# One encoder layer, two sequences: sequence 0's matrix memory takes the form of sequence 1's

## The chip, the cores and the metric

The kernel runs on one core of one Trainium2 chip. The metric is the time of one execution on the device, in microseconds (us). The time given for a kernel is the median of several runs. One more execution is taken with the hardware profiler; the page and the trace quoted here come from it.

## What is computed

The reference is one layer of a hybrid encoder over two independent sequences (`x_prompt`, `x_sample`) of 512 tokens and width 1024, all in float32. A half-step SwiGLU network is followed by a token-mixing block, a second SwiGLU network and a last RMSNorm. The mixing block feeds two branches from one projection: attention with 8 heads, and a bidirectional matrix memory (mLSTM) with 4 heads of width 128. Both are projected up, gated and merged:

```python
att = gqa_block_attention(aq, ak, av)
mem = mlstm_bidirectional(mq, mk, mv, gate_pre, mlstm_gate_bias, o_pre, mlstm_head_norm)
merged = jax.nn.sigmoid(g_att) * (att @ w_up_att) + jax.nn.sigmoid(g_mlstm) * (mem @ w_up_mlstm)
x = x + merged @ w_out
```

Unrolled over a whole sequence, one direction of one memory head is a masked score matrix with exponential decay weights, times the values, divided by a row normaliser:

```python
S_qk = jnp.einsum('bhtd,bhsd->bhts', qc, kc) * jnp.exp(D - m_t[..., None])
num = jnp.einsum('bhts,bhse->bhte', S_qk, vc) + w_inter[..., None] * jnp.einsum('bhtd,bhde->bhte', qc, C)
h = num / jnp.maximum(jnp.abs(den), jnp.exp(-m_t))[..., None]
```

The kernel forms the 512×512 weights of both directions directly, adds them, and multiplies by the values.

## The kernel before

**Arithmetic.** A float32 operand of a matmul is split into a high part (ScalarE, ACT: a copy that rounds) and a low part (VectorE, DVE: the difference), both in the type fp32r; `split` (L733, L734) does it for tiles, `split_w` (L284, L285) for weights. A product is then three matmuls: high·high, high·low, low·high. Each runs over 512 columns on TensorE (PE).

**The mixing block.** `mix(s, ...)` is a generator that runs once for each sequence s; it works with the tokens along the free axis, so that a head's q, k and values are 128-row tiles of 512 columns. A unit of work such as `mem_qk(h, j)` (q or k of head h), `att_gate(d)`, `merge_att(d)` or `mem_gate(d)` is a pair of a weight load and a computation; `go(...)` runs units in the order written, with loads ahead of computations. A scheduler then orders the instructions of each engine by their place in the code and by what is ready in its own model; inside `marks[0] = True` some instructions are pinned to the written order.

**One memory head, `mem_head(h)`.** For each of four row blocks i: three matmuls make the scores into a PSUM bank `pss` (L1309; two such banks); ACT makes five exponentials of decay rows (L1323); DVE multiplies scores and weights once for each direction (L1325). The decay rows come from DRAM by a DMA on SP's queue (L1088, `box<-ebuf`), and a masked copy `em` of them is made by an addition (L1091): on GpSimd (POOL) for heads 1 to 3 of sequence 0, on DVE otherwise. Then the normaliser is inverted and both directions are joined (L1336 ACT, L1337 and L1339 DVE). The result is four row tiles `Ts` of 128×512.

**Values, `mem_out(h)`.** The value product contracts over the columns of `Ts`, so they must be turned. Sequence 0 does it on PE: 16 transposes of 128×128 per head into `pst` (L1372), then `split`, then 12 matmuls into the bank `pso` (L1381). Sequence 1 does it without PE: `mem_blocks(h)` turns every 32×32 block in place on DVE (L1347, eight instructions per head), `mem_send` writes the blocks to DRAM in eight DMAs of 128 KB on POOL's queue (L1355, `tbuf`), and `mem_out` fetches four tiles `f` of 256 KB back in the turned order, also on POOL's queue (L1368). These are split and multiplied as above; an ACT copy (L1387) restores the order of the columns of `pso`. Then come the output gate (L1391), the sums of squares over a scratch row `turned_`, and the normed head into the tile `mem` (L1398).

**Order around it.** Sequence 1's four heads stand in one order written by hand: a head's scores, then units of other work, then that head's values. Sequence 0 runs a loop over the heads that puts units into a queue and takes them out with `fill`.

**Buffers.** `A(...)` takes one of seven equal large buffers; `att` (attention's output), `mem`, `Vm` (the values), `mg` (the gates), `kv` and `qT` live there. `F2()` takes one of four places for tiles of 128×512 (`f2`); attention's fetches, the scaled products of `mem_qk` of sequence 0 and the memory's fetches share them. Weights that are split live in four `w8` places, raw weights in four `wr` places. PSUM has banks `mm`, `pso`, `pss`, `pst`; merges and gates use `mm`.

Of the kernel before, what the change touches and what calls it, by code (L numbers as in the profile page):

```python
# [8 lines left out]
F32 = mybir.dt.float32  # L9
# [7 lines left out]
P = 128  # L17
# [9 lines left out]
def encoder(ctx, tc, I, outs):  # L27
# [837 lines left out]
    def mix(s, xh, xl, early=None, extra=None, after=None):  # L865
# [166 lines left out]

        def mem_qk(h, j):
            def done(pp):
                if j == 0 and not s:
                    t = wpool.tile([P, 4, S], F32R, tag="w8", bufs=4, name=nm("qk"))
                    qks[h] = [t[:, i] for i in range(4)]
                elif s:
                    t = mem[:, 2 + j] if h == 2 else wpool.tile([P, 2, S], F32R, tag="wr", bufs=4, name=nm("qk"))
                    qks.setdefault(h, []).extend(t[:, i] for i in range(2))  # L1040
                t = pp
                if not s:
                    t = F2()
# [40 lines left out]
        def mem_rows(h, d):  # L1084

            eb = T2(F32, "eb")
            eb3 = eb.rearrange("p (b s) -> p b s", b=4)
            nc.sync.dma_start(eb3, ebuf[d, :, h, :].partition_broadcast(P))  # L1088
            em = T2(F32, "eb")
            em3 = em.rearrange("p (b s) -> p b s", b=4)  # L1090
            (V_ if s or not h else G_).tensor_tensor(em3, eb3, tabs[3][:, d].unsqueeze(1).to_broadcast([P, 4, P]), op=ALU.add)  # L1091
            return eb3, em3

        def mem_scales():
# [246 lines left out]

        def mem_blocks(h, Ts):

            q = [wpool.tile([P, 8, 4, 32], F32, tag="wr", bufs=4, name=nm("qt")) for _ in range(2)]
            for i in range(4):
                for g in range(2):
                    V_.transpose(q[g][:, :, i, :],  # L1347
                                 Ts[i][0][:, g * 256:(g + 1) * 256].rearrange("p (n m) -> p n m", m=32))
            return h, q
# [9 lines left out]
        def mem_out(h, Ts):  # L1359
            moved = isinstance(Ts, int)  # L1360
            vm = Vm[0]
            po = PO()
            hs_ = slice(h * P, (h + 1) * P)
            turned = []
            for j in range(4 + 1):
                if j < 4 and moved:
                    p = F2()
                    mark(nc.gpsimd.dma_start(p, tbuf[Ts][4 * j:4 * j + 4].rearrange("c r a x -> (c r) (a x)")), True)  # L1368
                elif j < 4:
                    p = PT()  # L1370
                    for i in range(4):
                        nc.tensor.transpose(p[:, i * P:(i + 1) * P], Ts[i][0][:, j * P:(j + 1) * P], ident)  # L1372
                if j < 4:
                    ph, pl = T2(F32R), T2(F32R)
                    split(p, ph, pl)
                    turned.append((j, ph, pl))
                if j >= 1:
                    t, ph, pl = turned.pop(0)
                    with shifted(15):
                        for n, (a, b) in enumerate(((0, ph), (1, ph), (0, pl))):  # L1380
                            mark(nc.tensor.matmul(po, vm[:, a, t, hs_], b, start=(t == 0 and n == 0),  # L1381
                                                  stop=(t == 3 and n == 2)), True)
            h2 = T2()
            og = ogs[h]
            if moved:
                rows_ = T2()
                nc.scalar.activation(rows_.rearrange("p (i a m) -> p i a m", i=4, a=4),  # L1387
                                     po.rearrange("p (a i m) -> p i a m", i=4, a=4), AF.Copy)
                po = rows_
            nc.scalar.activation(h2, po, AF.Square)  # L1390
            V_.scalar_tensor_tensor(og, og, 1.0, po, op0=ALU.add, op1=ALU.mult)  # L1391
            turned_ = own[0] if own else F2()
            row = block_sums(h2, turned_)
            with shifted(60):
                rh = block_rstd(row, DM)
            with shifted(160):
                Rh = spread_rows(rh, turned_)
                V_.scalar_tensor_tensor(og, og, hn[:, h:h + 1], Rh, op0=ALU.mult, op1=ALU.mult)  # L1398
                split(og, mem[:, h, 0, :], mem[:, h, 1, :])

        if s:
            qk2, qk3 = [[mem_qk(h, j) for j in range(2)] for h in (2, 3)]
            ma = [merge_att(d) for d in range(KD)]
            marks[0] = True
            q = mem_blocks(0, mem_head(0))
            at = [mem_send(*q)]
            go(*mem_values(), *qk2)
            q = mem_blocks(1, mem_head(1))
            go(*qk3, ma[0], ma[1])
            mem_out(0, at[0])  # L1410
            at.append(mem_send(*q))
            q = mem_blocks(2, mem_head(2))
            go(att_gate(6), att_gate(7), ma[2], ma[3])
            mem_out(1, at[1])
            at.append(mem_send(*q))
            q = mem_blocks(3, mem_head(3))
            go(*ma[4:])
            mem_out(2, at[2])
            at.append(mem_send(*q))
            go(*[mem_gate(d) for d in range(EARLY)])  # L1420
            mem_out(3, at[3])
            marks[0] = False
        for h in range(HM if not s else 0):
            Ts = mem_head(h)
            if h == 0:
                go(*mem_values())
            queue.append(merge_att(2 * h))
            if h == 0:
                queue.append(merge_att(1))
            fill(1 + s)  # L1430
# [3 lines left out]
            if h:  # L1434
                queue.append(merge_att(2 * h + 1))
            fill(99)
# [559 lines left out]
```

## Time and profile before

| | |
|---|---|
| median of 3 runs | 2030.96 us (2028.93 to 2032.43) |
| the profiled execution | 2029.24 us |
| its span in the trace | 2027.5 us |
| mean granted clock of TensorE | 0.999 |
| DMA over the span | 482.11 MB, mean 238 GB/s |
| heads of sequence 0's memory in the trace | 797.5 to 955 us |
| heads of sequence 1's memory in the trace | 1188 to 1300 us |

The span is the stretch that the trace covers; the execution's own time is 1.7 us longer. In a row of the timeline the first two numbers are start and length in us, then engine, line, operation, output and inputs; what stands in brackets is the engine's idle time just before and what ended it. A busy time of PE counts matmuls from issue to a modelled end, so neighbouring ones overlap (a row says about 0.39 us where the next one starts 0.23 us later). A row that groups instructions ends with their busy time and the mean in ns, and behind the bar the idle time before them. "SPq" and "POOLq" are the queues' own instructions.

### The profile page before, as it was taken

To read this page: it belongs to the slowest core of one execution; us is meant where nothing else is said; L and a number is where in the kernel's file an instruction comes from. 1 tells how busy PE (TensorE), PEld (TensorE's weight loads), DVE (VectorE), ACT (ScalarE), POOL (GpSimd) and SP (SyncE) were. 2 spreads that over 40 slices of the span, in tenths; PEclk is the share of its full clock that TensorE was granted. 3 is DMA by queue.
4 is the path that set the end of the run, shared out by engine and by line. 5 is a ranking of instruction groups with operands and counts; after the bars stand their busy time and mean duration, and the time that the engine had idled before them with its cause. 6 is when DMAs were issued, how large, how long until landed. Compare 5 with 4: busy or idle time off the path is not lost.

```text
span 2027.5 us, 26874 instructions
## 1 busy us (share of the span) xinstructions
PE 2015.1 (99%) x9129; PEld 1661.4 (82%) x9129; DVE 1592.6 (79%) x2830; ACT 919.2 (45%) x1677; POOL 249.7 (12%) x313
## 2 busy tenths in 40 slices
PE   9999999999999999999999999999999999999998
PEld 7888888888888888788888878888888888888887
DVE  8989898896688788786566867377798988786797
ACT  7644444443224477653325655245444444442224
POOL 0243344201003000100120023011000000000001
PEclk9999999999999999999999999999999999999999
DMA  9778787799766766868657668867565655699753
GB/s 313 233 235 271 228 279 244 258 337 373 264 220 220 274 194 198 267 206 300 210 165 220 205 228 264 274 208 238 157 210 171 226 168 178 204 339 349 272 194 120
DMA packets 329546, 482.11 MB, mean 238 GB/s; under 512 B 23016, under 2 KB 196160, under 8 KB 328128
## 3 DMA queue, kind: packets, MB, share of 16 engines
q1 hardware_dynamic: 316352, 439.27, 64.9%
q0 software_dynamic: 12896, 40.86, 5.9%
q8 instruction: 72, 1.18, 0.2%
q14 instruction: 66, 0.54, 0.1%
q10 hardware_dynamic: 160, 0.27, 0.0%
HBM read 308.70 MB, written 171.61 MB: 237 GB/s over the span
## 4 chain that ended last, share of the span: by engine, by line
PE 94%; DVE 2%; DMA 2%; issue 1%; ACT 1%; SPq 0%; DVEq 0%; ACTq 0%
PE mm L856 16%; PE mm L380 11%; PE pso L380 11%; PE pst L380 11%; PE mm L650 9%; PE mm L842 5%; PE pss L380 5%; PE pss L650 4%; PE pst L650 4%; PE mm L821 3%; PE pso L650 3%; PE pss L1118 1%; PE pso L1165 1%; PE pso L1381 1%; PE pst L856 1%; PE pss L856 1%
## 5 line engine op out<-in xcount | busy, mean ns | idle before, releaser
L380 PE MATMUL pst<-xc,w 128*128 128x512 f32 x1056 | 253.8, 389 | 0.5 <-ACT t L415 0.5
L380 PEld LDWEIGHTS pst<-xc,w 128*128 128x128 f32 x1056 | 198.1, 188 | 42.0 <-ACT t L415 0.9
L380 PE MATMUL mm<-xc,w 128*128 128x512 f32 x972 | 229.8, 390 | 0.8 <-ACT t L388 0.8
L380 PEld LDWEIGHTS mm<-xc,w 128*128 128x128 f32 x972 | 181.8, 188 | 39.5 <-ACT t L388 1.9
L650 PE MATMUL mm<-rt,w 128*128 128x512 f32 x765 | 178.7, 389 | 0.0
L856 PE MATMUL mm<-xh,w 128*128 128x512 f32 x560 | 176.0, 391 | 0.0
L650 PEld LDWEIGHTS mm<-rt,w 128*128 128x128 f32 x765 | 143.5, 188 | 29.8
L338 ACT ACTIVATE w<-t 128x512 fp32r<-128x512 f32 x176 | 107.6, 628 | 130.7 <-issue 59.1
L339 DVE TENSOR_TENSOR w<-t,w 128x512 fp32r<-128x512 f32 x176 | 120.2, 701 | 31.7 <-ACT w L338 30.0
L380 PE MATMUL pso<-xc,f 128*128 128x512 f32 x528 | 127.1, 390 | 0.1
L380 PE MATMUL pss<-xc,w 128*128 128x512 f32 x528 | 126.8, 389 | 0.0
L380 PE MATMUL pso<-xc,w 128*128 128x512 f32 x528 | 126.8, 389 | 0.0
L856 PEld LDWEIGHTS mm<-xh,w 128*128 128x128 f32 x560 | 104.9, 188 | 21.8
L380 PEld LDWEIGHTS pso<-xc,f 128*128 128x128 f32 x528 | 98.9, 188 | 21.5 <-DVE t L419 1.1
L380 PEld LDWEIGHTS pss<-xc,w 128*128 128x128 f32 x528 | 99.1, 188 | 20.6
L380 PEld LDWEIGHTS pso<-xc,w 128*128 128x128 f32 x528 | 99.1, 188 | 20.6
L842 PE MATMUL mm<-xh,w 128*128 128x512 f32 x336 | 110.5, 395 | 0.0
L856 PE MATMUL mm<-xl,w 128*128 128x512 f32 x280 | 109.6, 391 | 0.0
L733 ACT ACTIVATE w<-wr 128x512 fp32r<-128x512 f32 x72 | 45.1, 632 | 138.3 <-PE pso L650 70.6
L733 ACT ACTIVATE w<-t 128x512 fp32r<-128x512 f32 x82 | 51.8, 632 | 107.4 <-PE pst L650 62.4
L650 PE MATMUL pss<-rt,w 128*128 128x512 f32 x396 | 93.7, 389 | 0.0
L650 PE MATMUL pst<-rt,w 128*128 128x512 f32 x396 | 93.7, 389 | 0.0
(464 smaller groups left out, 4168.1 us busy)
## 6 DMA issues: line engine op xcount, KB each, us to landing
rt<-rbuf SPq DMA_DIRECT2D x154, 512.0 KB, 5.8
w<-wpark SPq DMA_DIRECT2D x112, 512.0 KB, 5.1
wpark<-w SPq DMA_DIRECT2D x64, 512.0 KB, 3.6
wr<-in_ffn_w_gate_dram SPq DMA_DIRECT2D x62, 512.0 KB, 5.5
wr<-in_ffn_w_up_dram SPq DMA_DIRECT2D x44, 512.0 KB, 4.8
rbuf<-f SPq DMA_DIRECT2D x86, 256.0 KB, 4.3
rbuf<-R SPq DMA_DIRECT2D x82, 256.0 KB, 4.7
rbuf<-tab SPq DMA_DIRECT2D x74, 256.0 KB, 3.9
```

The lines of the kernel that those rows point to most:

```text
L338: pin(nc.scalar.activation(t[:, 0], src, AF.Copy))
L339: pin(V_.tensor_tensor(t[:, 1], src, f(t[:, 0]), op=ALU.subtract))
L380: nc.tensor.matmul(p, a[:, k, :], xt[:, b, k, :], start=(first and k == 0 and i == 0), stop=(k == HK_ - 1 and i == 2), skip_group_check=True)
L650: nc.tensor.matmul(p, u[:, a, d * P:(d + 1) * P], r[:, b, ts], start=(first and q == 0 and k == 0), stop=(q == len(us) - 1 and k == 2), sk ...
L733: nc.scalar.activation(hi, src, AF.Copy)
L821: mark(nc.tensor.matmul(p[b][:, :N], a[:, k, bs], w_[:, kl, :], start=(k == 0 and i == 0), stop=(k == KD - 1 and i == 2)), (kl, b, i) == ( ...
L842: pin(nc.tensor.matmul(p[0], a[:, k, :], b, start=(k == 0 and i == 0), stop=(k == n - 1 and i == 2)))
L856: mark(nc.tensor.matmul(p, a[:, k, :], b, start=(k == 0 and i == 0), stop=last), last)
L1118: pin(nc.tensor.matmul(p, qT[:, h, b * P:(b + 1) * P], kv[:, hk * 2 + j, :], start=(j == 0), stop=(j == 1)))
L1165: pin(nc.tensor.matmul(pos[h], Vst[:, kb, h // 4, :], w, start=(kb == KBS[0] and i == 0), stop=(kb == KBS[3] and i == 1)))
L1381: mark(nc.tensor.matmul(po, vm[:, a, t, hs_], b, start=(t == 0 and n == 0), stop=(t == 3 and n == 2)), True)
```

## The change

Sequence 0's matrix memory is done as sequence 1's is: one written order for both, the block turns on DVE, the passage through DRAM, and six gate units (`EARLY`) ahead of the last head's values. Its blocks do not use `wr` places but a large tile of their own, `broken` (three pairs of block tiles in rotation, and one row as the scratch `own`). The em additions all go to DVE. Of sequence 0's q and k, head 2's go into the tile `mem`, the others into `w8` places.

```diff
-                if j == 0 and not s:
+                if j == 0 and not s and h != 2:
                     t = wpool.tile([P, 4, S], F32R, tag="w8", bufs=4, name=nm("qk"))
                     qks[h] = [t[:, i] for i in range(4)]
-                elif s:
+                elif s or h == 2:
                     t = mem[:, 2 + j] if h == 2 else wpool.tile([P, 2, S], F32R, tag="wr", bufs=4, name=nm("qk"))
...
-            (V_ if s or not h else G_).tensor_tensor(em3, eb3, tabs[3][:, d].unsqueeze(1).to_broadcast([P, 4, P]), op=ALU.add)
+            V_.tensor_tensor(em3, eb3, tabs[3][:, d].unsqueeze(1).to_broadcast([P, 4, P]), op=ALU.add)
...
-        own = [T2(F32, "R")] if s else []
+        if s:
+            own = T2(F32, "R")
+        else:
+            blocks = A([P, 8, S], F32, "broken")
+            broken = blocks[:, 0:6].rearrange("p (q a) (n i m) -> p q (a n) i m", a=2, i=4, m=32)
+            own = blocks[:, 6]
...
-            q = [wpool.tile([P, 8, 4, 32], F32, tag="wr", bufs=4, name=nm("qt")) for _ in range(2)]
+            if s:
+                q = [wpool.tile([P, 8, 4, 32], F32, tag="wr", bufs=4, name=nm("qt")) for _ in range(2)]
+            else:
+                q = [broken[:, (2 * h + g) % 3] for g in range(2)]
...
-        if s:
-            qk2, qk3 = [[mem_qk(h, j) for j in range(2)] for h in (2, 3)]
...
-        for h in range(HM if not s else 0):
-            Ts = mem_head(h)
-            if h == 0:
-                go(*mem_values())
-            queue.append(merge_att(2 * h))
...
-            mem_out(h, Ts)
-            if h + 2 < HM:
-                queue.extend([att_gate(h + 6), mem_qk(h + 2, 0), mem_qk(h + 2, 1)])
...
+        qk2, qk3 = [[mem_qk(h, j) for j in range(2)] for h in (2, 3)]
+        ma = [merge_att(d) for d in range(KD)]
+        marks[0] = True
+        q = mem_blocks(0, mem_head(0))
+        at = [mem_send(*q)]
+        go(*mem_values(), *qk2)
+        q = mem_blocks(1, mem_head(1))
+        go(*qk3, ma[0], ma[1])
+        mem_out(0, at[0])
+        at.append(mem_send(*q))
+        q = mem_blocks(2, mem_head(2))
+        go(att_gate(6), att_gate(7), ma[2], ma[3])
+        mem_out(1, at[1])
+        at.append(mem_send(*q))
+        q = mem_blocks(3, mem_head(3))
+        go(*ma[4:])
+        mem_out(2, at[2])
+        at.append(mem_send(*q))
+        go(*[mem_gate(d) for d in range(EARLY)])
+        mem_out(3, at[3])
+        marks[0] = False
...
-        go(*[mem_gate(d) for d in range(EARLY * s, KD)])
+        go(*[mem_gate(d) for d in range(EARLY, KD)])
```

The lines from L1300 on stand five to eight lines lower in the changed kernel: the scores are L1314 there, their products with the weights L1330, the block turns L1355, the sends L1363, the fetches L1376, the value matmuls L1389, the ACT copy L1395, the gate product L1399. The order of instructions differs only in sequence 0's matrix memory. PE has 9065 matmuls instead of 9129, the 64 transposes gone.

First place, PE in the changed kernel around head 2's scores (`att` is attention's output; `mm_880_8091` is the eighth and last merge, `mm_884_8113` the first `mem_gate`, `mem_707_7054` holds head 2's q and k):

```order
L856 MATMUL mm_859_7998<-att_467_5977,w_856_7978 128x512 x9
L856 MATMUL mm_880_8091<-att_467_5977,w_856_7978 128x512 x12
L856 MATMUL mm_884_8113<-xh_341_5029,w_878_8085 128x512
L856 MATMUL mm_884_8113<-xl_342_5030,w_878_8085 128x512
L856 MATMUL mm_884_8113<-xh_341_5029,w_878_8085 128x512 x2
L856 MATMUL mm_884_8113<-xl_342_5030,w_878_8085 128x512
L856 MATMUL mm_884_8113<-xh_341_5029,w_878_8085 128x512
L1314 MATMUL pss_795_7610<-mem_707_7054 128x512
L1314 MATMUL pss_798_7623<-mem_707_7054 128x512
```

Before, head 2's scores came ahead of the last merges (its q and k were in a place of their own, `qk_771_7453`):

```order
L856 MATMUL mm_822_7735<-xh_341_5029,w_817_7699 128x512
L1309 MATMUL pss_825_7769<-qk_771_7453 128x512 x3
L1309 MATMUL pss_828_7782<-qk_771_7453 128x512 x3
L856 MATMUL mm_840_7843<-att_467_5977,w_787_7531 128x512 x2
L1309 MATMUL pss_831_7795<-qk_771_7453 128x512 x3
```

Head 2's scores have moved behind all eight merges, since `mem` has the large buffer in which `att` was. From the first of them to the first value matmul of head 2, PE now has 90 matmuls.

Second place, POOL's queue in the changed kernel. The first four rows fetch head 0's turned tiles, then come head 1's sends and fetches. The numbers ahead of the last ones in `f2_...` name the tiles; `f2_778` and `f2_784` have the same of the four places, as have `f2_781` and `f2_787`:

```order
L1376 DMA f2_778_7535<-tbuf0_259 128x512
L1376 DMA f2_781_7541<-tbuf0_259 128x512
L1376 DMA f2_784_7550<-tbuf0_259 128x512
L1376 DMA f2_787_7559<-tbuf0_259 128x512
L1363 DMA tbuf1_260<-broken_708_7055 32x8x128 x8
L1376 DMA f2_821_7791<-tbuf1_260 128x512
```

and DVE's rows that read the two other places, with head 2's scaled products, for the last time; they stand behind the evacuation of the last merge:

```order
L1275 SCALAR_TENSOR_TENSOR mg_377_5414<-mg_377_5414,mm_880_8091 128x512
L734 TENSOR_TENSOR mem_707_7054<-f2_746_7325,mem_707_7054 128x512
L734 TENSOR_TENSOR mem_707_7054<-f2_764_7441,mem_707_7054 128x512
```

Before, POOL had six em additions here and no transfer for sequence 0's memory. Now all fetches of heads 0 and 1 pass through two places while the other two are held. PE's value matmuls of head 0 stand among merges and gates:

```order
L856 MATMUL mm_7520<-att_5977,w_7485 128x512 x12
L856 MATMUL mm_7692<-att_5977,w_7485 128x512 x4
L1389 MATMUL pso_7534<-t_779_7537,Vm_7283 128x512 x2
L856 MATMUL mm_7692<-att_5977,w_7485 128x512
L1389 MATMUL pso_7534<-t_780_7538,Vm_7283 128x512
L856 MATMUL mm_7692<-att_5977,w_7485 128x512 x7
L856 MATMUL mm_7714<-xh_5029,w_7686 128x512
L1389 MATMUL pso_7534<-t_782_7543,Vm_7283 128x512 x2
```

The rows `mm_7520` and `mm_7692` are the first two merges, `t_779` and `t_780` the high and low half of the first fetched tile. The second piece is wanted 12 matmuls after the first.

Third place, DVE behind head 0's scores, where the low halves of the weights of the value projection are made (L285). Before:

```order
L285 TENSOR_TENSOR w_7172<-wr_7170,w_7172 128x1024
L1325 SCALAR_TENSOR_TENSOR t_719_7103,dn_7059<-pss_7099,t_719_7103 128x512
L1325 SCALAR_TENSOR_TENSOR t_720_7109,dn_7059<-pss_7099,t_720_7109 128x128
L1329 SCALAR_TENSOR_TENSOR dn_7059<-dn_7059 128x8
L1330 TENSOR_TENSOR dn_7059<-dn_7059,st_5417 128x8
```

In the changed kernel, where `w_7189` is the weight that was `w_7172`:

```order
L1330 SCALAR_TENSOR_TENSOR t_720_7104,dn_7060<-pss_7100,t_720_7104 128x512
L1330 SCALAR_TENSOR_TENSOR t_721_7110,dn_7060<-pss_7100,t_721_7110 128x128
L1334 SCALAR_TENSOR_TENSOR dn_7060<-dn_7060 128x8
L1091 TENSOR_TENSOR box_5409<-box_5409,tab_4349 128x512
L1335 TENSOR_TENSOR dn_7060<-dn_7060,st_5417 128x8
L285 TENSOR_TENSOR w_7189<-wr_7187,w_7189 128x1024
```

The low half of this weight has moved behind the last products of scores and weights and behind an em addition, which waits for its row from DRAM.

More of the change, by code (lines that the diff above doesn't have):

```diff
@@ L1391, in mem_out @@
             V_.scalar_tensor_tensor(og, og, 1.0, po, op0=ALU.add, op1=ALU.mult)
-            turned_ = own[0] if own else F2()
+            turned_ = own
             row = block_sums(h2, turned_)
@@ L1399, in mem_out @@
                 split(og, mem[:, h, 0, :], mem[:, h, 1, :])
-        if s:
-            qk2, qk3 = [[mem_qk(h, j) for j in range(2)] for h in (2, 3)]
[L1403 to L1422, printed above, removed]
@@ L1423, in mix @@
-        for h in range(HM if not s else 0):
-            Ts = mem_head(h)
-            if h == 0:
-                go(*mem_values())
-            queue.append(merge_att(2 * h))
-            if h == 0:
-                queue.append(merge_att(1))
-            fill(1 + s)
-            mem_out(h, Ts)
-            if h + 2 < HM:
-                queue.extend([att_gate(h + 6), mem_qk(h + 2, 0), mem_qk(h + 2, 1)])
-            if h:
-                queue.append(merge_att(2 * h + 1))
-            fill(99)
+        qk2, qk3 = [[mem_qk(h, j) for j in range(2)] for h in (2, 3)]
```

## The prediction

> **What bounds the kernel now.** The page comes first: the busy line and the chain that ended last.
>
> ```profile
> span 2027.5 us, 26874 instructions
> PE 2015.1 (99%) x9129; PEld 1661.4 (82%) x9129; DVE 1592.6 (79%) x2830; ACT 919.2 (45%) x1677; POOL 249.7 (12%) x313
> PE 94%; DVE 2%; DMA 2%; issue 1%; ACT 1%; SPq 0%; DVEq 0%; ACTq 0%
> ```
>
> TensorE is the bound, 99% busy. A change pays by taking matmuls from PE and costs what it makes PE wait. The stretch that the change touches comes next (columns: window, length, busy time of PE, PEld, DVE, ACT and POOL, granted clock, DMA share, GB/s), with PE's only two idle spells in it.
>
> ```profile
> 797.50:955.00 157.50, 156.40 (x725) 126.65 (x724) 118.51 (x266) 87.00 (x177) 8.21 (x6) 1.00 0.76 255
> 812.54 0.97 PE L1309 MATMUL pss<-qk 128*128 128x512 f32 x3 [0.70 <-DVE t L1325]
> 854.72 0.93 PE L1309 MATMUL pss<-qk 128*128 128x512 f32 x3 [0.40 <-DVE t L1325]
> ```
>
> PE idles 1.1 us of 157.5, so there is almost no waiting to win, while every new wait counts in full. One full matmul costs 0.227 us: (156.4 − 6.3 for the 64 small ones priced next) / 661.
>
> **What leaves PE.** All 64 transposes of sequence 0 go.
>
> ```profile
> L1372 PE MATMUL pst<-ident,t x64: 270/272/328, 828.3 to 916.2; 128*128 128x128 f32 x64
> 828.33 1.04 PE L1372 MATMUL pst<-ident,t 128*128 128x128 f32 x8
> 829.12 1.17 PE L856 MATMUL mm<-att,w 128*128 128x512 f32 x4
> ```
>
> The first row is from a listing whose starts match these. Matmuls overlap, so the price is start to start: (829.12 − 828.33) / 8 = 0.099 us, times 64 = 6.3 us. The 0.40 us wait at 854.72 I count as gone too, since head 1's scores move. **Gain 6.7 us.** Nothing else leaves PE.
>
> **What comes in, and where it hides.** The rows are sequence 1's, where the form runs already; they are grouped over 1188 to 1300 us.
>
> ```profile
> L1347 DVE STREAM_TRANSPOSE qt<-t 128x256 f32<-128x256 f32 x32 | 11.6, 419 | 0.0
> L1387 ACT ACTIVATE t<-pso 128x512 f32<-128x512 f32 x4 | 2.4, 598 | 7.5 <-PE pso L1381 7.5
> L733 ACT ACTIVATE t<-f 128x512 fp32r<-128x512 f32 x16 | 9.1, 621 | 0.1
> L734 DVE TENSOR_TENSOR t<-f,t 128x512 fp32r<-128x512 f32 x16 | 10.5, 687 | 16.9 <-ACT t L733 16.9
> L1391 DVE SCALAR_TENSOR_TENSOR box<-box,t 128x512 f32<-128x512 f32 x4 | 2.8, 693 | 6.3 <-ACT t L1387 6.3
> L1091 DVE TENSOR_TENSOR box<-box,tab 128x512 f32<-128x512 f32 x6 | 4.1, 690 | 6.0 <-DMA box<-ebuf 5.9
> L1381 PE MATMUL pso<-t,Vm 128*128 128x512 f32 x48 | 12.4, 395 | 0.0
> ```
>
> 32 turns are 11.6 us of DVE, 4 copies 2.4 us of ACT, six em adds 4.1 us of DVE. DVE is busy 118.5 of 157.5 us and PE has matmuls ready, so by volume this hides, at nothing; without that cover it would be at most DVE's sum, 16 us. The last row shows that sequence 1's 48 value matmuls made PE wait 0.0 us: the form can be free if PE has enough other work between a head's scores and its value matmuls. Sequence 1 has 36.4 us there for head 2 (scores from 1225.63, value matmuls from 1262.03; rows below). The order shown ahead gives sequence 0 less, and here the terms begin.
>
> **Head 2, the largest term.** The blocks tile makes one more claim on the seven large buffers, and `mem` gets the one that held `att`. Head 2's q and k now live in `mem`, so they are first written after the last merge of attention; the PE list shows head 2's scores behind it. From head 2's first score to its first value matmul PE's list holds 90 matmuls, 90 × 0.227 = 20.4 us. The chain that must fit into it, in sequence 1:
>
> ```profile
> 1225.63 1.52 PE L1309 MATMUL pss<-mem 128*128 128x512 f32 x6
> 1236.66 0.69 DVE L1091 TENSOR_TENSOR box<-box,tab 128x512 f32<-128x512 f32 x1 [1.03 <-DMA box<-ebuf]
> 1242.56 4.64 POOL L1355 DMA_DIRECT2D tbuf<-qt  x8 [17.50 <-DVE qt L1347]
> 1248.70 1.12 POOL L1368 DMA_DIRECT2D f<-tbuf  x2 [1.50 <-DMA tbuf<-qt]
> 1253.89 1.06 POOL L1368 DMA_DIRECT2D f<-tbuf  x2 [4.07 <-DMA tbuf<-qt]
> 1262.24 4.64 POOL L1355 DMA_DIRECT2D tbuf<-qt  x8 [7.29 <-DVE qt L1347]
> 1262.03 0.61 PE L1381 MATMUL pso<-t,Vm 128*128 128x512 f32 x2
> 1270.77 1.11 POOL L1368 DMA_DIRECT2D f<-tbuf  x2 [3.88 <-DVE row L232]
> L1368 POOL DMA_DIRECT2D f<-tbuf x16: 537/546/572, 1203.0 to 1272.6; - x16
> DMA to landing us min/median/max: 3.0/5.8/9.1
> ```
>
> Scores to first send 16.9 us; the two em adds in it and their wait (2 × 0.69 + 1.03 = 2.4) stand elsewhere in sequence 0, so 14.5. Sends to first fetch 6.1 (head 2) to 8.5 (head 3); I take 7.0, nearer the one that waits for DMA alone. Landing 5.8, split on ACT 0.6. Together 27.9 against 20.4: **wait 7.5 us**. The second pair of fetches was 5.2 us behind the first, and the third piece's matmuls come 1.4 us after the first's; I take **1.0 us** more, as the landings overlap, 0 to 3.8. Ends for the first piece: 14.5 + 6.1 + 3.0 + 0.6 gives 3.8; 16.9 + 8.5 + 9.1 + 0.6 gives 14.7.
>
> Behind it: PE's next gate product needs a PSUM bank whose reader stands on DVE behind head 2's four splits and its output product (L1391, now L1399). After the last value matmul come the ACT copy 0.6, the product 0.69 and the reader 0.69, while PE holds nothing it may start: **2.1 us** with handoffs; 0 if DVE gets to the bank while PE still waits for the pieces.
>
> **Heads 0 and 1, a ring with two places.** The `f2` ring has four places. Head 2's two products wait in two of them until `mem` is free, so the eight fetches of heads 0 and 1 pass through the other two. Count from E, the end of the last q/k product. The list needs the four pieces at E+3.6, 6.3, 7.9 and 11.1 (16, 28, 35 and 49 matmuls). A fetch costs 0.5 to issue, 5.8 to land, 0.6 for the high half; its place comes free 0.7 later. Place B is free about E+2 (DVE's scaling of the product 0.7, high half 0.6, low half 0.7), place A one product of 24 matmuls, 5.4 us, earlier, at E−3.5. High halves: E+3.5 by A, E+9 by B, then A again E+11.3, B again E+16.7. Waits: 0, 2.7, 0.7, 2.2. **5.6 us.** With landings of 3.0 all four are in time, 0; with 9.1, 12.
>
> Head 1: its third fetch needs the place of the first, whose low half stands on DVE behind the evacuation of merge 2. Counted from head 0's last value matmul, merge 2 ends at 10.2 (45 matmuls); evacuation 0.7, a weight's low half 1.2 and the split 0.7 with handoffs make 13.2. The third high half comes at 13.2 + 0.5 + 5.8 + 0.6 = 20.1 and is wanted at 17.0 (75 matmuls); the fourth loses 0.4 more: **3.5 us**, 0.6 to 7 by the landing's ends.
>
> **The em adds on DVE.** Before, POOL waited for their row; now DVE does, and the low halves of weights stand behind.
>
> ```profile
> 815.68 0.37 SPq L1088 DMA_DIRECT2D box<-ebuf  x1
> 819.25 1.32 POOL L1091 TENSOR_TENSOR box<-box,tab 128x512 f32<-128x512 f32 x1 [21.81 <-DMA box<-ebuf]
> 816.93 1.22 DVE L285 TENSOR_TENSOR w<-wr,w 128x1024 fp32r<-128x1024 f32 x1 [0.52 <-ACT w L284]
> 818.29 0.42 PE L821 MATMUL mm<-w,xh 128*128 128x512 f32 x1
> DMA to landing us min/median/max: 3.1/5.9/7.8
> ```
>
> The last row is the landing of all 16 such transfers (L1088). The low half ended at 818.15, just ahead of PE's next matmul on that weight. Now the add for head 1 stands ahead of it: 819.25 + 0.69 + 1.22 = 821.2, and PE reaches it four matmuls later than before by its list, near 819.2: **2.0 us**. With the shortest landing, 3.1, it is 1.5, and 0 if the transfer starts earlier; with 7.8 it is 6. The later adds stand ahead of weights that are wanted many matmuls later: nothing.
>
> **The queues.** The 32 sends (4.64 us for eight) and 16 fetches join POOL, whose 8.2 us of work in this stretch are the adds that leave it. A head's sends stand there behind the fetches of the head before; that is in the sums. SP issues the same rows. The new traffic, 32 × 128 KB + 16 × 256 KB = 8.4 MB in 157 us, is +53 GB/s on 255. Sequence 1's stretch is the nearest row to that sum of 308:
>
> ```profile
> 1188.00:1300.00 112.00, 111.38 (x489) 90.56 (x488) 73.68 (x220) 48.73 (x119) 27.31 (x48) 1.00 0.84 283
> L1325 DVE SCALAR_TENSOR_TENSOR t<-pss,t 128x512 f32<-128x512 f32 (+3 forms) x26 | 12.0, 485 | 2.1 <-ACT t L1323 2.0
> L1337 DVE SCALAR_TENSOR_TENSOR t<-t,dn,t 128x128 f32<-128x128 f32 x16 | 5.2, 334 | 0.0
> L1339 DVE TENSOR_SCALAR t<-t,dn 128x384 f32<-128x384 f32 (+2 forms) x12 | 3.9, 350 | 0.1
> ```
>
> At 283 GB/s the fetches landed in those 5.8 us, so I take their median.
>
> **Sum.** 7.5 + 1.0 + 2.1 + 5.6 + 3.5 + 2.0 − 6.7 = **+15.0 us**. The profiled execution took 2029.24 us, 1.7 below the median of 2030.96. On it 2044.2; on the median 2046.0. I forecast 2045.
>
> **Rivals.**
> *Transfers short: no change.* With every landing at 3.0 and the quickest send the waits are 0 + 0.6 + 3.8 + 2.1 = 6.5 us, against 6.7: about 2030. For it: 3.0 occurs. Against: it is the shortest of 16, at less traffic than here. 0.15.
> [...]
> *Head 2's chain short: faster.* The 14.5 us from scores to sends hold other work of DVE in sequence 1. Its own is (12.0 + 5.2 + 3.9 + 11.6) / 4 = 8.2 us by the rows above. If DVE comes to it at once, the chain is 8.2 + 6.1 + 5.8 + 0.6 = 20.7, and head 2 waits 0.3 instead of 8.5; with landings of 3.0 for heads 0 and 1 as well, 0.6 + 2.1 are left: 3.0 − 6.7 = −3.7, and −6.7 if the bank is read early: 2023 to 2026. It decides from a chain of 20.4 us. For it: the 0.0 of sequence 1. Against: weights' low halves stand between in DVE's list, and head 3's scores too. 0.11.
> *Saturated DMA: slower still.* If 308 GB/s pushes landings to 9.1, the waits are 14.7 + 12 + 7 + 2.1 + 6 = 42 us, +35, about 2065. It decides from landings of some 8 us. Against: 283 GB/s gave 5.8. 0.12.
> *The change doesn't do what it says.* PE's list has none of the 64 transposes, so this is closed: 0.
> *A slow clock after the waits.* The first matmuls of the span, after idleness:
>
> ```profile
> 1.63 2.93 PE L1468 MATMUL pst<-xc 128*128 128x512 f32 x6 [1.63 <-DVE xc L1553]
> ```
>
> They took 0.49 us each instead of 0.227. If a wait of 7.5 us brings that back for some 10 matmuls, it is +2.6 us, about 2048, inside the forecast's own range.
> [...]
>
> **Chances.** Forecast 0.62 (2036 to 2058), no change 0.15, faster 0.11, saturated 0.12; so faster 0.11, same 0.15, slower 0.74, where 0.2%, some 4 us, is about what a measurement can tell from no change. The range leaves out the faster case and half of the saturated one: 2026 to 2061.
>
> **What would show it.** Right, step by step: 9065 matmuls instead of 9129; PE idle before head 2's value matmuls some 7 us and before head 0's in pieces of 1 to 3, each released by a split (L733, L734) of a tile just fetched; PE idle some 2 us for a bank after head 2; DVE idle on box<-ebuf ahead of the third value weight. Wrong: PE waiting next to nothing at the value matmuls, fetches landing in 3 us, or most of PE's new waits standing outside this stretch.

## The result, and the profile after

The changed kernel takes 2059.85 us (median of 4 runs, 2057.9 to 2060.18), the kernel before 2029.95 us (4 runs): 1.0146 times as long, 95% interval 1.0128 to 1.0163, or 30 us more. The forecast was 2045 us and a range of 2026 to 2061. The profiled execution took 2057.9 us. First the page of the changed kernel (called after from here on): span, busy line, chain that ended last.

```profile
span 2056.1 us, 26865 instructions
PE 2018.4 (98%) x9065; PEld 1659.0 (81%) x9065; DVE 1603.8 (78%) x2868; ACT 922.4 (45%) x1681; POOL 267.8 (13%) x355
PE 90%; DMA 4%; DVE 3%; ACT 2%; issue 1%; SPq 0%; POOL 0%; DVEq 0%; ACTq 0%; POOLq 0%
```

The 64 transposes are gone, and yet PE is busy 3 us longer, though with 64 instructions fewer; its share of the chain has fallen from 94% to 90%. The reason for both shows in the stretch that the prediction looked at, now in after (same columns):

```profile
797.50:955.00 157.50, 131.41 (x529) 100.47 (x528) 107.92 (x255) 78.81 (x165) 26.30 (x46) 0.91 0.81 257
```

PE idles 26 us where it idled 1, and the granted clock, which was 1.00, is 0.91. These are PE's waits in the timeline of after that were not there before:

```profile
817.90 0.50 PE L1314 MATMUL pss<-qk 128*128 128x512 f32 x1 [0.32 <-DVE t L1330]
820.95 0.49 PE L821 MATMUL mm<-w,xh 128*128 128x512 f32 x1 [1.09 <-DVE w L285]
856.71 0.88 PE L856 MATMUL mm<-att,w 128*128 128x512 f32 x2 [2.36 <-ACT w L284]
857.97 4.66 PE L856 MATMUL mm<-att,w 128*128 128x512 f32 x14 [0.38 <-DVE w L285]
869.33 1.22 PE L1389 MATMUL pso<-t,Vm 128*128 128x512 f32 x2 [3.89 <-ACT t L733]
894.22 1.28 PE L1389 MATMUL pso<-t,Vm 128*128 128x512 f32 x3 [3.11 <-DVE t L734]
902.17 0.73 PE L1389 MATMUL pso<-t,Vm 128*128 128x512 f32 x2 [0.79 <-ACT t L733]
942.50 3.09 PE L1389 MATMUL pso<-t,Vm 128*128 128x512 f32 x6 [8.94 <-ACT t L733]
947.42 2.88 PE L1389 MATMUL pso<-t,Vm 128*128 128x512 f32 x6 [1.82 <-ACT t L733]
952.38 0.79 PE L856 MATMUL mm<-xh,w 128*128 128x512 f32 x1 [2.07 <-DVE t L889]
```

From top to bottom: the third value weight (two rows, the first at a score matmul just ahead of it), the first merge's weight (high half, low half), head 0's values, head 1's (two rows of three), head 2's (two rows), the bank behind head 2. In what follows a wait is counted from the start of the matmul before, less the 0.227 us that one takes, since ends are modelled; so the row with 8.94 counts 9.1. Two rows of the value matmuls show the second thing: six matmuls at 942.50 are given 3.09 us, six at 0.227 would have about 1.5. The same window view, cut finer:

```profile
942.00:946.00 4.00, 3.09 (x6) 1.57 (x6) 1.38 (x2) 1.08 (x2) 1.46 (x3) 0.51 1.00 351
952.00:955.00 3.00, 2.62 (x6) 2.14 (x7) 2.70 (x5) 1.52 (x3) 0.38 (x1) 0.50 1.07 378
958.00:965.00 7.00, 7.00 (x33) 5.79 (x32) 4.78 (x11) 2.10 (x3) 0.00 (x0) 1.00 0.69 248
```

In these windows behind the waits the granted clock of TensorE was 0.51 and 0.50, and from 958 to 965 us it was 1.00 again. 31 matmuls of the stretch take 0.427 us from their own start to the next one's instead of 0.227, six more are partly slow: 31 × 0.2 + 2.2 = 8.4 us.

| term of the sum | forecast, us | measured, us |
|---|---|---|
| 64 transposes and one wait that go | −6.7 | −6.9 |
| third value weight | 2.0 | 1.7 |
| head 0's values | 5.6 | 4.1 |
| head 1's values | 3.5 | 4.8 |
| head 2's values | 8.5 | 11.3 |
| bank behind head 2 | 2.1 | 2.6 |
| first merge's weight | 0 | 3.2 |
| matmuls at half clock | not in the sum | 8.4 |
| all | +15.0 | +29.2 |

The spans differ by 28.6 us. So a wait stands at every place that was named, 24.5 us in all instead of 21.7, and 11.6 us were not in the sum.

### The profile page after: what moved, and what is told of

Same layout as the page of the kernel before. It is cut to its first block, busy times and chain, and to the rows that moved or that the text cites. A ratio compares the mean times of both kernels' runs of the same rounds, so it can differ in the third digit from the quotient of the medians.

```text
span 2056.1 us, 26865 instructions
## 1 busy us (share of the span) xinstructions
PE 2018.4 (98%) x9065; PEld 1659.0 (81%) x9065; DVE 1603.8 (78%) x2868; ACT 922.4 (45%) x1681; POOL 267.8 (13%) x355
## 4 chain that ended last, share of the span: by engine, by line
PE 90%; DMA 4%; DVE 3%; ACT 2%; issue 1%; SPq 0%; POOL 0%; DVEq 0%; ACTq 0%; POOLq 0%
PE mm L856 13%; PE pso L380 11%; PE pst L380 11%; PE mm L380 10%; PE mm L650 8%; PE pss L380 6%; PE mm L842 5%; PE pss L650 4%; PE pst L650 4%; PE mm L821 3%; PE pso L650 3%; PE pss L1118 1%; PE pso L1165 1%; PE pst L856 1%; PE pss L856 1%; DMA f<-tbuf 1%
## 5 line engine op out<-in xcount | busy, mean ns | idle before, releaser
L380 PEld LDWEIGHTS pso<-xc,f 128*128 128x128 f32 x528 | 98.9, 188 | 21.7 <-DVE t L419 1.3
```

Source lines behind the costliest of these rows:

```text
L380: nc.tensor.matmul(p, a[:, k, :], xt[:, b, k, :], start=(first and k == 0 and i == 0), stop=(k == HK_ - 1 and i == 2), skip_group_check=True)
```

## Experiments

### One part undone each

`e1_w8` puts head 2's q and k back into a `w8` place, `e2_pool` the em additions back on POOL, `e5_wr` the blocks into `wr` places:

```diff
# e1_w8
-                if j == 0 and not s and h != 2:
+                if j == 0 and not s:
-                elif s or h == 2:
+                elif s:
# e2_pool
-            V_.tensor_tensor(em3, eb3, ...
+            (V_ if s or not h else G_).tensor_tensor(em3, eb3, ...
# e5_wr
-                q = [broken[:, (2 * h + g) % 3] for g in range(2)]
+            q = [wpool.tile([P, 8, 4, 32], F32, tag="wr", bufs=4, name=nm("qt")) for _ in range(2)]
-            turned_ = own
+            turned_ = own if s else F2()
```

> Of the change, one thing is undone: head 2's q and k go into a w8 place, as heads 0, 1 and 3's do, and not into mem. Theory A (the waits come from mem having the buffer of att, which holds head 2's scores back to the last merge and two of the four f2 places until then): PE's list now has 170 matmuls, 38.6 us, between head 2's scores and its values, and the f2 ring has its four places. The waits at the value matmuls of heads 0, 1 and 2 (4.1 + 4.8 + 11.3 us) and at the bank behind head 2 (2.6) fall to under 5 in all, and the slow matmuls behind them (some 8 us) go with them: 2028 to 2036 us. Rival B (the turns' way through DRAM is too long wherever it stands, because 8.4 MB more traffic slows the landings): PE still waits 10 us or more at the value matmuls, 2045 to 2060. Rival C (places for weights): the w8 place that head 2 takes is missed by the weights, and PE waits instead at gates and merges for their halves, above 2040.

> Of the change, one thing is undone: the em additions of sequence 0's heads 1 to 3 are on POOL again. Theory A: only the wait at the third value weight (1.75 us) goes, and the one at the first merge's weight (3.2 us) becomes shorter by DVE's 1.2 us of waiting for a row; the waits at the value matmuls stay. 2055 to 2058 us. Rival D (the additions on DVE delay everything behind them, head 0's and head 1's blocks too): 2045 or less, with shorter waits at the value matmuls of head 0 and 1.

> Of the change, the tile of the blocks' own is undone: sequence 0's blocks go through wr places as sequence 1's do, and the scratch row is an f2 place, as before. mem then has the buffer that kv had, and PE's list has head 2's scores 62 matmuls ahead of head 0's values. Theory A: the waits at the value matmuls of heads 0 to 2 fall to under 5 us in all; but blocks and raw weights now share four places, so weights may come late. 2028 to 2042 us. Rival B (the way through DRAM is too long wherever it stands): 10 us or more of waits at the value matmuls, 2045 to 2060.

Measured: `e1_w8` 2037.61 us, ratio to before 1.004 (1.0025 to 1.0055); `e2_pool` 2061.05 (1.0158; 1.0143 to 1.0173); `e5_wr` 2089.21 (1.0301; 1.0284 to 1.0318). PE's longer waits in `e1_w8`:

```profile
823.28 0.50 PE L821 MATMUL mm<-w,xh 128*128 128x512 f32 x1 [1.02 <-DVE w L285]
859.10 0.73 PE L856 MATMUL mm<-att,w 128*128 128x512 f32 x2 [1.44 <-ACT w L284]
871.07 1.22 PE L1389 MATMUL pso<-t,Vm 128*128 128x512 f32 x2 [4.43 <-ACT t L733]
946.09 0.73 PE L1389 MATMUL pso<-t,Vm 128*128 128x512 f32 x2 [2.37 <-ACT t L733]
```

One tile in another place takes 22 of the 30 us away. The waits of heads 1 and 2 and of the bank are gone; head 0's 4.6 us stay, under the 5 that theory A allowed for the four. Rival B's 10 us and rival C's 2040 us are not reached. But the first merge's weight still waits (2.3 us), head 3 (the last row) now does, and the time is 2 us above theory A's range.

`e2_pool` loses the wait at the third value weight, and the first merge's weight waits 1.6 us instead of 3.2, but PE waits 7.8 us for head 1's values instead of 4.8. It ends 3 us above theory A's range, and rival D falls. It does not price the additions, though, since on POOL they stand in the queue of the fetches:

```profile
888.85 3.87 POOL L1091 TENSOR_TENSOR box<-box,tab 128x512 f32<-128x512 f32 x2 [6.48 <-DMA box<-ebuf]
892.66 1.09 POOL L1376 DMA_DIRECT2D f<-tbuf  x2
```

Head 1's last two fetches go out behind two additions that waited for their rows, though the last of their places was empty at 889.4. In after the same additions stand on DVE, ahead of a low half of head 1:

```profile
889.40 0.69 DVE L1091 TENSOR_TENSOR box<-box,tab 128x512 f32<-128x512 f32 x1 [3.52 <-DMA box<-ebuf]
893.48 0.68 DVE L734 TENSOR_TENSOR t<-f,t 128x512 fp32r<-128x512 f32 x1
```

DVE stands still for 3.5 us, and the low half of head 1's first piece comes at 893.48, though ACT had its high half by 888.2. The longest of head 1's waits, 3.3 of the 4.8 us, is for this low half. So the additions delay head 1 in both kernels, by different ways; what they cost alone no run shows.

`e5_wr` shows what the tile of the blocks' own is for: at the value matmuls of heads 0 to 2 hardly a wait is left (0.4 us), as theory A has it, but in four shared places raw weights come late, and PE waits for halves of weights, 7.9 us in one place and 6.8 in another. Theory A's range for it was wrong: it named the late weights and gave them no price.

### The ring apart from the late scores

`f_hold` keeps head 2's scores where the change put them, behind the last merge, but holds the two products in a `w8` place, so that the ring has its four places.

```diff
+                    if h == 2 and j == 0:
+                        qks["raw"] = wpool.tile([P, 4, S], F32, tag="w8", bufs=4, name=nm("raw"))
-                    t = F2()
+                    t = qks["raw"][:, j] if h == 2 else F2()
```

> The changed kernel, with head 2's two products kept in a w8 place until mem is free, and not in two places of the f2 ring; head 2's scores stay behind the last merge, and the first matmuls of all four heads' values stand at the same count of PE's list as in the changed kernel but for head 1's (12 earlier). It separates the two halves of theory A. If the ring with two places made the waits of heads 0 and 1 (4.1 and 4.8 us in the changed kernel) and the late scores that of head 2 (11.3 and 2.6 behind it), then heads 0 and 1 wait under 4 us in all, head 2 and its bank still 12 to 15: 2050 to 2056 us. If both came from the late scores, or from transfers, heads 0 and 1 wait as before: 2058 or more.

Measured: 2052.07 us, ratio 1.011 (1.0093 to 1.0127), 8 us less than the changed kernel. Head 1's waits are gone; head 0 still waits 4.3 us, which is just over the 4 allowed for both heads, head 2 10.3 and 1.3, its bank 2.5. The first merge's weight no longer waits, but the weight of a q/k product now does (2.3 us). The ring shows in POOL's rows of after, the eight fetches of heads 0 and 1; five of them are put down to a split (L734) that empties a place:

```profile
856.73 0.57 POOL L1376 DMA_DIRECT2D f<-tbuf  x1 [25.53 <-DVE qk L734]
861.94 0.55 POOL L1376 DMA_DIRECT2D f<-tbuf  x1 [4.64 <-PE mm L856]
863.33 0.54 POOL L1376 DMA_DIRECT2D f<-tbuf  x1 [0.84 <-DVE t L734]
870.29 0.54 POOL L1376 DMA_DIRECT2D f<-tbuf  x1 [6.42 <-DVE t L734]
882.29 1.12 POOL L1376 DMA_DIRECT2D f<-tbuf  x2 [5.82 <-DVE row L246]
894.46 0.54 POOL L1376 DMA_DIRECT2D f<-tbuf  x1 [11.05 <-DVE t L734]
895.66 0.54 POOL L1376 DMA_DIRECT2D f<-tbuf  x1 [0.66 <-DVE t L734]
```

So the two halves of theory A are worth some 8 us (the ring) and, from `f_hold` to `e1_w8`, 14 us (the late scores). The 8 us are not the places alone: in `f_hold` DVE's list also has head 1's low half earlier, behind one em addition that waits 1.9 us instead of two and a wait of 3.5.

### What is left in `e1_w8`

Three kernels start from `e1_w8`: `f_t2` takes the products of heads 2 and 3 out of the ring, `f_order` has that and a new written order for sequence 0, `f_late` gives sequence 0's value matmuls a later place.

```diff
# f_t2, f_order
+                    t = T2() if h > 1 else F2()
# f_late
-                    with shifted(15):
+                    with shifted(15 if s else 150):
# f_order
-        go(*qk3, ma[0], ma[1])
+        go(*qk3, att_gate(6), att_gate(7), ma[0], ma[1])
-        go(att_gate(6), att_gate(7), ma[2], ma[3])
+        go(*ma[2:6])
-        go(*ma[4:])
+        go(*ma[6:], mem_gate(0))
-        go(*[mem_gate(d) for d in range(EARLY)])
+        go(*[mem_gate(d) for d in range(1, EARLY)])
```

> The kernel that gave 2037.6 (head 2's q and k in a w8 place), and the products of heads 2 and 3 in t2 places, so that no product of theirs stands in the ring before head 0's fetches. There PE still waited 4.6 us for head 0's last piece, whose fetch was issued at 863.2, after the last product had left its place. If that place was the cause, the wait falls under 1 us and the slow matmuls behind it go: 2031 to 2034. If the landing was (7 us for this one), the wait stays and the time is 2036 to 2040.

> The kernel that gave 2037.6, with a later place for sequence 0's value matmuls in the scheduler's order: 27, 20, 77 and 71 matmuls later for heads 0 to 3, nothing else changed by hand. If the waits that are left (4.6 us at head 0, 2.5 at head 3) are pieces that come a few us after the place the list gives them, they go, with their slow matmuls (3.4 us): 2027 to 2032. If PE's list has nothing to put in their place, the wait moves to the gates and merges behind: 2034 to 2040.

> The kernel of f_t2 with the two attention gates ahead of the first two merges, four merges between head 0's and head 1's values, and one gate of the memory before head 2's: head 0's values stand 46 matmuls, 10.4 us, later in PE's list, and the first merge's weight has 24 products more of time. If places in the list set the waits, those of head 0 (4.6 us) and of the first merge's weight (2.3) go: 2027 to 2032. If DVE and ACT, whose queues carry splits of weights and blocks, set them, other waits take their place: 2034 to 2040.

Measured: 2038.66 (1.004; 1.0025 to 1.0055), 2045.82 (1.0076; 1.006 to 1.0091) and 2040.53 us (1.0052; 1.0037 to 1.0067). None is better than `e1_w8`, and none of the hopes came true. In `f_t2` head 0's wait is gone, so under this load its place in the ring was what held it (`g_quiet`, below, has the same place without the load, and 1.7 us of the wait are left); but PE now waits 4.0 us at head 1's scores and 4.3 us for head 3's values. The wait that was removed came up elsewhere. What these two have in common shows in ACT's rows of `f_t2`, ahead of the waits:

```profile
842.70 1.06 ACT L284 ACTIVATE w<-wr 128x1024 fp32r<-128x1024 f32 x1 [3.92 <-DMA wr<-in_w_in_dram]
941.41 1.06 ACT L284 ACTIVATE w<-wr 128x1024 fp32r<-128x1024 f32 x1 [6.26 <-DMA wr<-in_w_up_mlstm_dram]
```

ACT stands still at the high half of a weight that has not landed, with exponentials and splits behind it in its order.

### The weights' transfers

The DMA issues of the window 797.5 to 955 us (median us to landing at the end) for the kernel before, the changed kernel, `e1_w8` and `g_quiet`, in one fence each:

```profile
wr<-in_w_in_dram SPq DMA_DIRECT2D x14, 512.0 KB, 6.4
wr<-in_w_up_att_dram SPq DMA_DIRECT2D x3, 512.0 KB, 6.0
```

```profile
wr<-in_w_in_dram SPq DMA_DIRECT2D x13, 512.0 KB, 8.1
wr<-in_w_up_att_dram SPq DMA_DIRECT2D x4, 512.0 KB, 9.2
```

```profile
wr<-in_w_in_dram SPq DMA_DIRECT2D x13, 512.0 KB, 9.0
wr<-in_w_up_att_dram SPq DMA_DIRECT2D x4, 512.0 KB, 11.1
f<-tbuf POOLq DMA_DIRECT2D x16, 256.0 KB, 6.5
```

```profile
wr<-in_w_in_dram SPq DMA_DIRECT2D x13, 512.0 KB, 5.0
f<-tbuf POOLq DMA_DIRECT2D x16, 256.0 KB, 4.1
```

and the window of `g_quiet`, in the columns of before:

```profile
797.50:955.00 157.50, 153.24 (x673) 122.62 (x672) 128.50 (x307) 90.47 (x183) 27.31 (x48) 1.00 0.61 185
```

Raw weights landed later in the kernels with the turns, by their medians from 6.4 us to 8.1 and 9.0. The kernel parks sequence 0's split weights in DRAM for sequence 1, 512 KB for each half. `g_quiet` is `e1_w8` without that in the stretch; `g_quiet_after` is the changed kernel, `g_quiet_before` the kernel before, with the same left out.

```diff
+        if quiet[0]:
+            skipped.add(key)
-        if not park:
+        if not park or key in skipped:
             return hi, lo
```

> The kernel that gave 2037.6 (head 2's q and k in a w8 place), and sequence 0's memory stretch without the transfers that park its split weights in DRAM (18 pairs of 512 KB, of the 45 MB in the window 797 to 955 us, where DMA's share is 0.87); sequence 1 loads and splits these weights again, which will cost it time of its own, so the stretch is read, not the whole. Contention (the form's 8.4 MB push the landing of raw weights from 6.4 to 9.0 us, and what waits for them on ACT holds up exponentials and splits behind it): in the stretch the landings of raw weights return to 7 us or less, and PE's waits of some 15 us fall to 6 or less. Order (ACT and DVE have too much ahead of the pieces, whatever the transfers): the waits stay above 10 us.

> The changed kernel with the same transfers left out, sequence 1 loading and splitting those weights again. Contention as a part of the changed kernel's waits: the wait at the first merge's weight (3.2 us) goes, the third value weight's (1.75) stays, the waits at the value matmuls of heads 0 to 2 become shorter by what landings shrink (1 to 2 us each) and stay above 10 us in all, since places and the late scores still set them. Theory A alone: all of them stay within 1 us, but for the merge's weight.

> The kernel before with the same transfers left out of its stretch: the control. Its PE waited 1.1 us there, so the stretch stays as long as it was, within 1 us; what the whole loses is sequence 1's price for splitting these weights again, 0 to 40 us. If contention is what is left in g_quiet, that kernel is as fast as this one or up to 6 us faster (the 64 transposes); if not, it is 5 to 10 us slower.

Measured: `g_quiet` 2091.0, `g_quiet_after` 2107.0, `g_quiet_before` 2092.87 us. All three load and split those weights again in sequence 1 (the control is 62 us slower than the kernel before), so they are compared with each other and in the stretch. In `g_quiet` the raw weights land in 5.0 us, PE's waits (those over 0.3 us) fall from 13.0 us in `e1_w8` to 5.1, of which 0.9 stood in before too, and no matmul is slow; the clock is 1.00. It is level with its control or a little ahead: the medians differ by 1.9 us, the ratios to before are 1.0292 (1.0277 to 1.0307) and 1.0303 (1.0286 to 1.0318). `e1_w8` itself was some 8 us slower than before. In `g_quiet_after` the merge's weight no longer waits, and heads 0, 1 and 2 wait 1.8, 1.6 and 6.7 us, 10 us less than in after, where 1 to 2 us less for each were expected; the bank behind head 2 keeps its 2.5. Head 2's 6.7 us stay without the load: this kernel is 16 us slower than `g_quiet`, from which it differs by head 2's q and k alone, and that is what the places and the late scores cost at a DMA share of 0.54. One thing is not separated here: the parking's transfers also stand in SP's queue, among the loads of raw weights, and wait there for the splits (51 us in `e1_w8` for high halves alone). The landing times count from the issue, and they fell from 9.0 to 5.0 us, so the load on DMA has its part; what the shorter queue gave beside it was not tried.

### The clock

Two kernels add matmuls whose results are not used, ahead of head 2's values: `e4_warm` 36, `h_warm` 56 and 14 more ahead of the third piece.

```diff
+                    if h == 2 and not s and t in (0, 2):
+                        busy = PT()
+                        with shifted(300):
+                            for _ in range(56 if t == 0 else 14):
+                                mark(nc.tensor.matmul(busy, vm[:, 0, 0, 0:P], xh[:, 0, :], start=True, stop=True), True)
```

> To the changed kernel 36 matmuls are added that compute nothing that is used, 36 x 0.227 = 8.2 us of PE work, just ahead of head 2's first value matmul, where PE idled 9.1 us; the rest of the order is the same. If the 0.427 us of the matmuls behind the waits are a clock that falls while PE is idle, the matmuls behind head 2 run at 0.227 for the most part (10 slow ones and four partly slow ones, 3.3 us, fall to 1 or less), and 8.2 us of added work make the kernel 1 to 3 us faster: 2056 to 2059. If they are slow for another reason (their operands, or DMA traffic), the slow ones stay and the time is the same or longer, 2060 or more.

> The changed kernel again with matmuls that compute nothing that is used, now enough to cover head 2's waits: 56 (12.7 us) ahead of its first value matmul and 14 (3.2 us) ahead of the third piece's, where the changed kernel's PE waited 9.1 and 2.2 us; the rest of PE's order is the same. If idleness is what halves the granted clock, the stretch behind head 2's first value matmul shows a granted clock near 1.00 and no matmul 0.427 us behind the one before it, but for what the bank's wait of 2.5 us brings on; the slow ones (3.3 us) go, and against 4.6 us of work beyond the waits the kernel takes 2059 to 2063. If DMA's load or the value matmuls themselves make them slow, the granted clock is 0.5 there again and the time is 2064 or more.

Measured: `e4_warm` 2060.16 us, no faster than the changed kernel: its 8.2 us of work did not last, as the pieces came 1.5 us later by themselves, PE still idled 2.4 and 2.8 us, and 23 matmuls of the stretch took 0.427 us. It decided nothing. `h_warm` took 2061.58 us, inside the 2059 to 2063 that were expected if idleness is the cause. Its windows around head 2's values (948.4 to 954.4 us):

```profile
946.00:950.00 4.00, 4.00 (x20) 3.30 (x19) 0.69 (x1) 0.59 (x2) 0.58 (x1) 1.00 1.03 366
950.00:955.00 5.00, 4.42 (x20) 3.34 (x18) 1.38 (x2) 1.64 (x3) 1.52 (x3) 1.00 1.01 307
955.00:962.00 7.00, 5.50 (x18) 4.48 (x19) 4.91 (x14) 2.64 (x5) 1.82 (x4) 0.76 0.98 353
```

With PE never idle the clock stays at 1.00 through head 2's values, at DMA shares of 1.01 to 1.03; it falls only behind the bank's wait of 2.1 us, which nothing fills, to a mean of 0.76 in the last window. 15.9 us of useless work made the kernel 1.7 us longer by the medians. In after, the first of these values ran at a granted clock of 0.51 behind 9.1 us of idleness, at a DMA share of 1.00 (942 to 946 us): what differs between the two runs is PE's idleness, not DMA's load.

## Why the prediction was right, and only half the size

The time lies in the range, 1 us from its end, and above the 2036 to 2058 of the forecast's own case; the loss is twice the forecast. The direction and most places of the waits came from the right mechanism. That the range held was partly luck, since 11.6 us came from outside the sum.

**The bound** was read rightly: PE idled 1.1 us, there was nothing to win but the transposes, and these gave the 6.3 us of the sum.

**Head 2** (forecast 8.5, measured 11.3). The mechanism was right, as `e1_w8` shows by removing it. In after, scores started at 912.74 and the list's 90 matmuls lasted to 933.4; the sends began at 926.30, the first fetch at 934.29, the first value matmul at 942.50. The steps are 13.6, 8.0 and 8.2 us where I had 14.5, 7.0 and 6.4: the DMA legs were undersized, since I took medians at a DMA share of 0.84, and from 930 to 942 us the share was 1.00.

**The bank** (2.1, measured 2.6) stands as forecast.

**Heads 0 and 1** (forecast 9.1, measured 8.9) agree in sum by luck. Head 0's pieces were to wait 0, 2.7, 0.7 and 2.2 us; the second waits 4.1 and the others nothing. Its fetch takes the place that the last product of head 3 leaves:

```profile
860.70 0.69 DVE L734 TENSOR_TENSOR qk<-f,qk 128x512 fp32r<-128x512 f32 x1
```

This place came free at 861.4, 7.2 us behind the last q/k product (it ended at 854.2) where I had 2; in `f_hold`, with four places, the last piece waits for the same place. For head 1 I had the third fetch as what makes PE wait, 3.5 us; that piece and the fourth wait 0.6 and 1.0 us, and 3.3 us are the low half of the first, behind the em addition.

**The em additions** (2.0, measured 1.7) were right at the third value weight. "The later adds stand ahead of weights that are wanted many matmuls later: nothing" was not: the one at 889.40 holds DVE for 3.5 us ahead of head 1's low half. `e2_pool` moved this wait to POOL's queue and was no faster.

**The step that failed** is the one on weights and queues: "The new traffic ... is +53 GB/s on 255", followed by "I take their median". I applied the traffic to the new transfers alone and not to the raw weights, whose landing rose from 6.4 to 8.1 us in after and holds up ACT and DVE in their order:

```profile
841.00 1.06 ACT L284 ACTIVATE w<-wr 128x1024 fp32r<-128x1024 f32 x1 [5.27 <-DMA wr<-in_w_in_dram]
842.09 1.23 DVE L285 TENSOR_TENSOR w<-wr,w 128x1024 fp32r<-128x1024 f32 x1 [4.69 <-DMA wr<-in_w_in_dram]
```

The first merge's own raw weight had landed by 844.0; ACT came to its high half at 855.6, behind a split that had waited 4.5 us for DVE. This cost 3.2 us, for which the sum had nothing. In `g_quiet_after`, without the parking, the wait is gone, and in `g_quiet` 13.0 us of waits fall to 5.1; with the em additions on POOL (`e2_pool`) half of the 3.2 us goes too, so both had a part in it.

**The clock** stood as a rival at +2.6 us, inside the range, "for some 10 matmuls"; it was 31 and six more, 8.4 us, the largest single miss. The error was to charge one wait. Each wait of 3 us or more in after, at 869, 894 and 942, had its own slow stretch behind it, and so had those of 2.5 and 2.6 us at 857 and 952. In `h_warm` 2.1 us of idleness were followed by a granted clock of 0.50 from 956.4 to 959.8 us.

**Short transfers** did not come about: the fetches' median was 6.4 us at a DMA share of 0.81 in after, 4.1 at 0.61 (`g_quiet`) and 6.5 at 0.87 (`e1_w8`). The prediction's sum for this rival had also left out the third value weight, 1.5 us at the shortest landing by its own row. **The saturated case** came half true: the fetches' median stayed under 8 us and the stretch moved 257 GB/s, not 308, but the raw weights' median was 8.1 us, and head 2's first fetch took 7.5. **The faster case** needed head 2's chain under 20.4 us; it took 29.8.

No version ran faster than the kernel before. `g_quiet` against `g_quiet_before` shows the form level with the transposes at a DMA share of 0.61 in the stretch; with the parking in place no order that was tried was level.

## What to carry to other kernels

A large tile that is added to a rotating pool changes which tile inherits whose buffer: look up who gets the buffer that comes free last, and whether a chain starts with writing there. In after, DVE waited 3.5 us for one transfer, and head 1's low half, which stood behind it in its list, came at 893.48 us though ACT had its high half by 888.2: price an added wait by what stands next in that list, too. Where PE is the bound, look for slow matmuls behind a wait: in after each wait of 3 us or more had another 1.3 to 2.4 us at a granted clock of 0.50 behind it, and the waits of 2.5 and 2.6 us had slow matmuls behind them too. New transfers can delay those that were there already: here the DMA share of the stretch was 0.76 before and 0.81 in after, and the median landing of raw weights rose from 6.4 to 8.1 us. Charge them to the weights, too.

## What the runs showed of the hardware

Fetches of 256 KB landed in 3.7 us at a DMA share of 0.54 (`g_quiet_after`), 4.1 at 0.61 and 6.5 at 0.87 (`e1_w8`), and raw weights of 512 KB in 4.5, 5.0 and 9.0 (medians; the shares are means over the window): landing times nearly doubled or doubled while the mean share rose from 0.54 to 0.87.

The clock's fall did not follow the length of a wait alone: behind 2.1 us of idleness at 956.50 in `h_warm` the granted clock was 0.50, and behind 2.2 us at 868.33 in `e2_pool` it was 1.00. In after it was 0.50 or 0.51 for 30.6 us in all between 857.1 and 956.1 us. Windows with their granted clocks, one of `h_warm`, one of `e1_w8` behind the wait at 946.09, and two of `e2_pool`:

```profile
956.40:959.80 3.40, 3.30 (x8) 2.63 (x9) 2.43 (x5) 1.89 (x3) 1.06 (x2) 0.50 1.04 379
947.10:950.50 3.40, 3.40 (x9) 2.63 (x9) 1.57 (x3) 0.51 (x1) 0.00 (x0) 0.50 1.02 348
866.60:870.00 3.40, 1.67 (x7) 1.24 (x7) 1.43 (x2) 2.13 (x3) 0.70 (x2) 1.00 0.62 230
870.00:873.40 3.40, 3.40 (x15) 2.55 (x14) 1.09 (x2) 0.25 (x2) 3.40 (x7) 1.00 1.02 295
```

What sets the two cases apart was not shown.
